# First norm's scale behind the transposes, handovers without GpSimd, and early splits of the next stage's first weights

## The chip, the cores and the metric

The kernel runs on one core of a Trainium2 chip. The metric is the device time of one execution in microseconds. Before the change it is 1447.9 us, the median of three runs that lie between 1447.25 and 1447.98.

## What is computed

A transformer block and two further layers, over 512 tokens of 1024 float32 features:

```python
def first_block(x, ...):
    h = rms_norm(x, pre_mix_g)                 # x * rsqrt(mean(x*x) + eps) * g
    proj = h @ w_in                            # 1024 x 8192
    ...                                        # two attentions, gated: mix
    x = x + rms_norm(mix @ w_mix_out, post_mix_g)
    h = rms_norm(x, pre_ffn_g)
    u = causal_depthwise_conv(h @ w_up, conv_w, conv_b)
    gate, val = jnp.split(u, 2, axis=-1)
    y = (jax.nn.gelu(gate, approximate=True) * val) @ w_down
    return x + rms_norm(y, post_ffn_g)

def second_block(x, ...):
    for l in range(2):
        h = rms_norm_2(x, norm_pre[l])
        proj = h @ w_in[l]                     # 1024 x 2732
        ...                                    # three attentions: mixed
        x = x + rms_norm_2(mixed @ w_out[l], norm_post[l])
    return x
```

## The kernel before, in words

Every float32 operand of a large product is split in two parts, hi (a cast on ScalarE) and lo (source minus hi, on VectorE); `mm3` then makes three matmuls for one, hi by hi, hi by lo and lo by hi. Weights come by DMA from SyncE's queue into `wraw` (three buffers) and `wsplit` makes `whi` and `wlo` (four buffers each). Activations are normalised with a token on each partition and then transposed on TensorE (`tp`), four tiles of 128 columns into one PSUM bank; `transpose_split` casts that bank into the hi part of `hT` on ScalarE and subtracts into its lo part on VectorE. There are four tiles of 128 tokens, t = 0 to 3, each with two halves of 512 features (u = 0, 1).

A stage ends in `post_norm`: the product with the output weights, for the last four k's held back (`LATE` = 4), so that tile 0 is finished first, then tile 1 and so on. `finish(t)` makes tile t's last products, the mean of squares (ScalarE squares with an accumulator, `mean_squares`; GpSimd makes v and then r = v to the power -1/2), y = product times r times gain (VectorE, one instruction for each half), the residual sum (half 0 on GpSimd, half 1 on VectorE), and then `after`, which is the next stage's `pre_norm`: squares of the sum, v and r, xn = x times r times gain (VectorE), transposes, splits. `in_steps` interleaves the tiles. There are three such handovers into a next stage: from the mix to the FFN, from the FFN to layer 0, from layer 0 to layer 1. `ahead`, set at the end of each `post_norm`, gives the next four weight splits an engine for their lo part: three of four go to GpSimd, and the last two wait until tile 1's hT is made.

The first product after a handover is `fm` for the FFN (a chunk of 128 columns of the gate or value half; the first two chunks in two halves of 256 tokens, so that tiles 0 and 1 suffice to begin) and `tm_full` for a layer (428 columns, two k's for one load).

At the start the gains of the first norm are spread over the partitions by two matmuls with a row of ones (`g_pre`), and matmuls on a zero tile (`keep_busy`, tile `idle`) run before and behind them, to no output. The first product (`pv`) makes the values of the first attention, in fours of 128 tokens.

Each engine takes its instructions in the order that the program has after scheduling, and a waiting instruction holds all behind it on its engine.

Of the kernel before, what the change touches and what calls it, by code (L numbers as in the profile page):

```python
# [94 lines left out]
def emit(tc, A, out):  # L95
# [9 lines left out]
    def f(t):  # L105
        return t.bitcast(F32)
# [77 lines left out]
    def wsplit(raw):  # L184
# [26 lines left out]
    def fm(W, pitch, base, c0, acts, kt=8, tag="pj", parts=1):  # L211

        hi, lo = wsplit(wtile(wcols(W, pitch, base, c0, 128, kt)))
        ps = bank(tag, "fm")
        n = 512 // parts
        for u in range(0, 512, n):
            for k in range(kt):
                ah, al = acts(k)
                mm3(ps[:, u:u + n], hi[:, k], lo[:, k], ah[:, u:u + n], al[:, u:u + n],
                    k == 0, k == kt - 1)  # L220
# [11 lines left out]
    def transpose_split(src, k0, t, hT, sp_tag="t"):  # L232
# [9 lines left out]
    def pre_norm(xt, t, g, hT, pool):  # L242
# [4 lines left out]
        for u in range(2):  # L247
            normed[t] = nc.vector.scalar_tensor_tensor(xn[u], xt[u], r, g[u], op0=OP.mult,
                                                       op1=OP.mult).ins
        yield  # L250
        for u in range(2):
            transpose_split(xn[u], u * 4, t, hT, "pj" if t == 1 else "t")
# [33 lines left out]
    def tm_full(W, pitch, base, kt, acts, tags, c0, w, kstep):  # L286

        banks = [bank(tg, "tm") for tg in tags]
        for s in range(0, kt, kstep):
            hi, lo = wsplit(wtile(wrows(W, pitch, base, s, kstep, c0, w)))  # L290
            for k in range(kstep):
                ah, al = acts(s + k)
                for t in range(4):
                    mm3(banks[t][:, :w], ah[:, t * 128:(t + 1) * 128],
                        al[:, t * 128:(t + 1) * 128], hi[:, k], lo[:, k],
                        s + k == 0, s + k == kt - 1)
        return banks

    def post_norm(W, base, kt, act, g, resid, pool, after, last=False):
# [23 lines left out]
        def finish(t):  # L323
# [978 lines left out]
```

## Time and profile before

| what | value |
|---|---|
| time, median of three runs | 1447.9 us |
| profiled execution's own time | 1448.2 us |
| its span, first to last instruction | 1446.4 us |
| TensorE busy | 1428.5 us, 99% of the span |
| VectorE busy | 805.8 us, 56% |
| ScalarE busy | 635.1 us, 44% |
| GpSimd busy | 119.5 us, 8% |
| mean granted TensorE clock | 0.998 |

The profiled execution is one run of the same program. PE is TensorE, DVE is VectorE, ACT is ScalarE, POOL is GpSimd, SP is SyncE. Behind an operation stand the tile that it writes and those that it reads; a line number is that of the program. In a timeline, what stands in brackets is the idle time in front of an instruction and the instruction that ended it. A float32 matmul on the idle tile, and one that spreads the gains, leaves two records in the trace.

### The profile page before, as it was taken

The page shows a single profiled execution, that of the slowest core. Times are in us where ns is not written, and L with a number is a line of the kernel's source. Part 1 is how long each engine was busy: PE and PEld are TensorE (multiplying, and loading weights), DVE is VectorE, ACT ScalarE, POOL GpSimd, SP SyncE. Part 2 cuts the span into 40 slices and gives each one's busy share as a digit, 9 for nine tenths or more (in the row PEclk, how much of TensorE's full clock was granted, in tenths as well). Part 3 has the DMA queues.
Part 4 walks back from the last instruction along what each step waited for, and adds up shares of the span by engine and source line. Part 5 has one row for each costly group of instructions (what it writes and reads, how often), then busy time and mean ns, then how long its engine had stood idle before and what let it go on. Part 6 is the DMA issues. An engine that isn't in the chain of part 4 may idle for free.

```text
span 1446.4 us, 19576 instructions
## 1 busy us (share of the span) xinstructions
PE 1428.5 (99%) x7384; PEld 1153.2 (80%) x7384; DVE 805.8 (56%) x1559; ACT 635.1 (44%) x1346; POOL 119.5 (8%) x188
## 2 busy tenths in 40 slices
PE   9999999999999999999999999999999989999998
PEld 7778878887888888888888888876777777767776
DVE  6454367555434465655554335657666376575745
ACT  4444443333322354433333324536666353475643
POOL 1000000000000060000000004500000064000000
PEclk9999999999999999999999999999999999999999
DMA  5664345432333526433342332633111315311111
GB/s 180 169 170 118 86 110 140 108 94 74 106 101 97 176 75 108 117 102 91 99 131 87 102 97 64 182 105 88 30 45 59 101 46 121 80 44 44 59 45 73
DMA packets 212360, 141.91 MB, mean 98 GB/s; under 512 B 39383, under 2 KB 191971, under 8 KB 212266
## 3 DMA queue, kind: packets, MB, share of 16 engines
q1 hardware_dynamic: 212266, 140.67, 35.1%
q8 instruction: 58, 0.95, 0.3%
q14 instruction: 36, 0.29, 0.1%
HBM read 129.08 MB, written 5.00 MB: 93 GB/s over the span
## 4 chain that ended last, share of the span: by engine, by line
PE 93%; POOL 3%; DVE 1%; ACT 1%; DMA 1%; issue 1%; SPq 0%; DVEq 0%; POOLq 0%; ACTq 0%
PE fm L207 17%; PE fm L208 17%; PE fm L209 17%; PE tm L207 6%; PE tm L209 6%; PE tm L208 6%; PE pt L861 3%; PE pv L207 2%; PE pv L209 2%; PE pv L208 2%; PE oA L866 2%; PE S L948 1%; PE S L1166 1%; PE S L949 1%; PE oC L866 1%; PE oM L866 1%
## 5 line engine op out<-in xcount | busy, mean ns | idle before, releaser
L207 PE MATMUL fm<-hT,whi 128*128 128x512 f32 (+1 forms) x1056 | 407.4, 386 | 1.5 <-DVE hT L175 1.4
L208 PE MATMUL fm<-hT,whi 128*128 128x512 f32 (+1 forms) x1056 | 408.0, 387 | 0.0
L209 PE MATMUL fm<-hT,wlo 128*128 128x512 f32 (+1 forms) x1056 | 407.2, 386 | 0.0
L175 DVE TENSOR_TENSOR wlo<-wraw,whi 128x1024 fp32r<-128x1024 f32 (+1 forms) x209 | 245.7, 1177 | 259.3 <-ACT whi L174 248.1
L174 ACT CAST whi<-wraw 128x1024 fp32r<-128x1024 f32 (+2 forms) x218 | 219.5, 1009 | 324.0 <-PE fm L208 238.2
L207 PEld LDWEIGHTS fm<-hT,whi 128*128 128x128 f32 x1056 | 198.3, 188 | 41.4 <-DVE hT L175 1.6
L209 PEld LDWEIGHTS fm<-hT,wlo 128*128 128x128 f32 x1056 | 198.6, 188 | 39.8 <-issue 1.8
L208 PEld LDWEIGHTS fm<-hT,whi 128*128 128x128 f32 x1056 | 198.7, 188 | 39.3 <-issue 1.7
L208 PE MATMUL tm<-wlo,ah 128*128 128x512 f32 x368 | 143.7, 391 | 0.0
L209 PE MATMUL tm<-whi,al 128*128 128x512 f32 x368 | 143.0, 390 | 0.0
L207 PE MATMUL tm<-whi,ah 128*128 128x512 f32 x368 | 139.1, 392 | 0.0
L864 ACT COPY PT<-pt 128x512 f32<-128x512 f32 (+1 forms) x104 | 51.3, 521 | 79.5 <-PE pt L861 73.8
L207 PEld LDWEIGHTS tm<-whi,ah 128*128 128x128 f32 x368 | 69.1, 188 | 14.6 <-issue 0.7
L209 PEld LDWEIGHTS tm<-whi,al 128*128 128x128 f32 x368 | 69.1, 188 | 14.3 <-issue 0.2
L208 PEld LDWEIGHTS tm<-wlo,ah 128*128 128x128 f32 x368 | 69.1, 188 | 14.0
L272 POOL TENSOR_SCALAR post_v<-post_ss 128x1 f32<-128x1 f32 x16 | 9.3, 583 | 763.0 <-ACT y L268 642.3
L789 DVE SCALAR_TENSOR_TENSOR u<-fm,cw,u 128x511 f32<-128x511 f32 x88 | 65.4, 746 | 8.6 <-ACT u L786 7.2
L891 ACT ACTIVATE P<-P,nm 128x256 f32<-128x256 f32 (+3 forms) x96 | 53.5, 561 | 21.7 <-DVE nm L887 21.4
L861 PE MATMUL pt<-ident,P 128*128 128x128 f32 x352 | 56.7, 284 | 0.0
L861 PEld LDWEIGHTS pt<-ident,P 128*128 128x128 f32 x352 | 38.0, 141 | 20.2 <-issue 18.2
L207 PE MATMUL pv<-whi,hT 128*128 128x512 f32 x128 | 51.3, 406 | 0.0
L209 PE MATMUL pv<-whi,hT 128*128 128x512 f32 x128 | 51.2, 403 | 0.0
(280 smaller groups left out, 1948.5 us busy)
## 6 DMA issues: line engine op xcount, KB each, us to landing
wraw<-in_w_in_dram SPq DMA_DIRECT2D x100, 512.0 KB, 4.3
wraw<-in_w_up_dram SPq DMA_DIRECT2D x44, 512.0 KB, 4.0
wraw<-in_w_down_dram SPq DMA_DIRECT2D x22, 512.0 KB, 3.6
wraw<-in_w_out_dram SPq DMA_DIRECT2D x16, 512.0 KB, 3.5
rs<-rq SPq DMA_DIRECT2D x48, 128.0 KB, 2.3
xt<-in_x_dram SPq DMA_DIRECT2D x16, 256.0 KB, 6.4
wraw<-in_w_mix_out_dram SPq DMA_DIRECT2D x8, 512.0 KB, 3.9
w<-in_cmp_w_dram SPq DMA_DIRECT2D x32, 128.0 KB, 3.6
```

The source lines that it names most:

```text
L174: a = nc.scalar.copy(hi, src)
L175: return a, engine.tensor_tensor(out=lo, in0=src, in1=f(hi), op=OP.subtract)
L207: nc.tensor.matmul(ps, ah, bh, start=first, stop=False)
L208: nc.tensor.matmul(ps, ah, bl, start=False, stop=False)
L209: nc.tensor.matmul(ps, al, bh, start=False, stop=last)
L789: nc.vector.scalar_tensor_tensor(u[:, d:], ps[:, :T - d], cw[:, j, c:c + 1], u[:, d:], op0=OP.mult, op1=OP.add)
L861: nc.tensor.transpose(pt[:, o + i * 128:o + i * 128 + 128], p, ident)
L864: nc.scalar.copy(at[:, :o], pt[:, :o])
L866: nc.tensor.matmul(O[ROWS[r], c0:c0 + w], v(r, kb), at[:, o:o + w], start=start, stop=stop)
L891: nc.scalar.activation(t[:, c:c + w], t[:, c:c + w], AF.Exp, bias=nm[:, u:u + 1], scale=-1.0, accum_out=den[:, u:u + 1])
L948: nc.tensor.matmul(ps[:, :w], q[:, s], kh[:, k0:k0 + w], start=True, stop=False)
L949: nc.tensor.matmul(ps[:, :w], q[:, s], kl[:, k0:k0 + w], start=False, stop=True)
```

## The change

- **The start.** The gains are loaded as eight rows of 128, transposed once to a column for each block of 128 features (`gT`), and multiplied in behind the transposes: xn is now only x times r (half 0 a copy with a scale on ScalarE, half 1 on VectorE), and VectorE multiplies the transposed bank by the columns back into xn, from where hT's parts are split. The row of ones, the two spreading matmuls and the eight idle matmuls behind them go; the idle matmuls at the head become twelve in place of nine.
- **The handovers.** The residual sum of half 0 moves from GpSimd to VectorE, and all weight splits have their lo part on VectorE. Nothing waits for tile 1's hT any more.
- **Early splits.** Ahead of `finish`, the first weights of the next stage (chunk 0 of gate and value for the FFN; k = 0 to 3 of the 428 columns for a layer) are loaded and split into tiles `wh` and `wl` that lie with the activations, so that they don't take the four held buffers. The other weights are split as before.

```diff
     def wsplit(raw):
...
-        engine, t = ahead.pop(0) if ahead else (nc.vector, None)
-        with ExitStack() as queued:
-            for ins in evacuated[t] if t is not None else ():
-                queued.enter_context(tc.issue_after(ins))
-            split(raw, hi, lo, engine)
+        split(raw, hi, lo)
         return hi, lo
...
+    def split_k(src, hi, lo):
+        hi, lo = [a[:, :src.shape[1] * src.shape[2]].rearrange("p (k n) -> p k n", k=src.shape[1])
+                  for a in (hi, lo)]
+        split(src, hi, lo)
+        return [(hi[:, k], lo[:, k]) for k in range(src.shape[1])]
...
     def transpose_split(src, k0, t, hT, sp_tag="t", gT=None):
...
+        if gT is not None:
+            h = src.rearrange("p (a b) -> p a b", a=4)
+            i = nc.vector.tensor_tensor(
+                h, ps, gT[:, k0:k0 + 4][:, :, None].to_broadcast([128, 4, 128]), op=OP.mult)
+            scaled.setdefault(t, []).append(i.ins)
+            ps = h
...
     def pre_norm(xt, t, g, hT, pool, gT=None):
...
+        if gT is None:
+            for u in range(2):
+                nc.vector.scalar_tensor_tensor(xn[u], xt[u], r, g[u], op0=OP.mult, op1=OP.mult)
+        else:
+            scaled[t] = [nc.scalar.activation(xn[0], xt[0], AF.Copy, scale=r).ins]
+            nc.vector.tensor_scalar(xn[1], xt[1], r, None, op0=OP.mult)
...
         def finish(t):
...
-                    (nc.vector if u else nc.gpsimd).tensor_tensor(out=res[u], in0=res[u],
-                                                                  in1=ys[u], op=OP.add)
+                    nc.vector.tensor_add(res[u], res[u], ys[u])
...
+        first = ready()
         in_steps([finish(t) for t in range(4)], SKEW)
-        ahead[:] = [(nc.gpsimd, None), (nc.gpsimd, None), (nc.vector, 1), (nc.gpsimd, 1)]
+        return first
...
-    keep_busy(9)
+    keep_busy(12)
     xt = [load_x(0)]
...
-    for u in range(2):
-        spread = nc.tensor.matmul(g_pre[u], grow[:, D:], grow[:, u * 512:u * 512 + 512],
-                                  start=True, stop=True)
-    with tc.issue_after(spread.ins):
-        keep_busy(8)
+    ps = bank("t", "gT")
+    nc.tensor.transpose(ps[:, 0:8], g8, ident[0:8, 0:8])
+    gT = small("gT", 8, 1)
+    nc.vector.tensor_copy(gT, ps[:, 0:8])
...
+    def up_weights():
+        res = []
+        for c0 in (0, DFF):
+            raw = wtile(wcols(A["w_up"], 2 * DFF, 0, c0, 128))
+            res.append(split_k(raw[:, 0:4], c2("wh", F32R), c2("wl", F32R))
+                       + split_k(raw[:, 4:8], c2("wh", F32R), c2("wl", F32R)))
+        return res
...
+    def layer_weights(l):
+        res = []
+        for k0 in (0, 2):
+            raw = wtile(wrows(W2, PW2, l * D * PW2, k0, 2, A_G, 428))
+            for k in range(2):
+                res += split_k(raw[:, k:k + 1], c2("wh", F32R), c2("wl", F32R))
+        return res
```

How the instructions stand: at the start, on TensorE, before the change (`tp_161` and `tp_168` are tile 0's two banks, `tp_186` is tile 1's first; a row with x8 stands for eight alike):

```order
L381 MATMUL idle_81<-z_80 128x128 x9
L397 MATMUL g_pre_103<-grow_97 128x512 x2
L381 MATMUL idle_81<-z_80 128x128 x8
L236 MATMUL tp_161<-ident_72,xn_136 128x128 x4
L236 MATMUL tp_168<-ident_72,xn_137 128x128 x4
L236 MATMUL tp_186<-ident_72,xn_145 128x128 x4
L207 MATMUL pv_240<-whi_242,hT0_78 128x512
L208 MATMUL pv_240<-wlo_243,hT0_78 128x512
L236 MATMUL tp_193<-ident_72,xn_146 128x128 x4
L209 MATMUL pv_240<-whi_242,hT1_79 128x512
```

and with it (`tp_156` and `tp_164` are tile 0's banks, `tp_183` is tile 1's first):

```order
L399 MATMUL idle_81<-z_80 128x128 x12
L413 MATMUL gT_105<-ident_72,g8_100 128x8
L240 MATMUL tp_156<-ident_72,xn_131 128x128 x4
L240 MATMUL tp_164<-ident_72,xn_132 128x128 x4
L200 MATMUL pv_243<-whi_245,hT0_78 128x512
L201 MATMUL pv_243<-wlo_246,hT0_78 128x512
L202 MATMUL pv_243<-whi_245,hT1_79 128x512
...
L200 MATMUL pv_243<-whi_261,hT0_78 128x512
L240 MATMUL tp_183<-ident_72,xn_140 128x128 x4
```

The gain matmuls and eight idle ones are gone, tile 0's first six products stand ahead of tile 1's transposes, and the second weights (`whi_261`) come before those.

At the handover to the FFN, on VectorE, from tile 2's y on, before (`xt` is the residual; `hT1` is the lo part of hT, from tile 0's two banks and then tile 1's two):

```order
L347 SCALAR_TENSOR_TENSOR y_4282<-tm_3970,post_r_4291,g_post_3944 128x512
L347 SCALAR_TENSOR_TENSOR y_4283<-tm_3971,post_r_4291,g_post_3944 128x512
L349 TENSOR_TENSOR xt_3957<-xt_3957,y_4283 128x512
L175 TENSOR_TENSOR hT1_3965<-tp_4231,hT0_3964 128x4x128
L175 TENSOR_TENSOR hT1_3965<-tp_4238,hT0_3964 128x4x128
L175 TENSOR_TENSOR hT1_3965<-tp_4293,hT0_3964 128x4x128
L175 TENSOR_TENSOR hT1_3965<-tp_4300,hT0_3964 128x4x128
```

and with the change (`wlo_4542` and `wlo_4601` are chunk 1's gate and value weights, `wlo_4663` is chunk 2's gate; `tp_4254` and `tp_4261` are tile 0's banks, `tp_4316` is tile 1's first):

```order
L365 SCALAR_TENSOR_TENSOR y_4305<-tm_3973,post_r_4314,g_post_3947 128x512
L365 SCALAR_TENSOR_TENSOR y_4306<-tm_3974,post_r_4314,g_post_3947 128x512
L172 TENSOR_TENSOR wlo_4542<-wraw_4539,whi_4541 128x1024
L367 TENSOR_TENSOR xt_3959<-xt_3959,y_4305 128x512
L367 TENSOR_TENSOR xt_3960<-xt_3960,y_4306 128x512
L172 TENSOR_TENSOR wlo_4601<-wraw_4598,whi_4600 128x1024
L172 TENSOR_TENSOR wlo_4663<-wraw_4660,whi_4662 128x1024
L172 TENSOR_TENSOR hT1_3968<-tp_4254,hT0_3967 128x4x128
L172 TENSOR_TENSOR hT1_3968<-tp_4261,hT0_3967 128x4x128
L172 TENSOR_TENSOR hT1_3968<-tp_4316,hT0_3967 128x4x128
L172 TENSOR_TENSOR hT1_3968<-tp_4323,hT0_3967 128x4x128
L259 SCALAR_TENSOR_TENSOR xn_4334<-xt_3959,pre_r_4365,g_ffn_3949 128x512
```

Three weight splits and one more add stand ahead of hT's first lo part. The first product of the FFN reads the lo parts of tile 0 and tile 1 out of the first bank of each.

At the handover to layer 1, on VectorE, from tile 1's xn on, before:

```order
L248 SCALAR_TENSOR_TENSOR xn_9612<-xt_3952,pre_r_9643,g_pre_9325 128x512
L248 SCALAR_TENSOR_TENSOR xn_9613<-xt_3953,pre_r_9643,g_pre_9325 128x512
L349 TENSOR_TENSOR xt_3957<-xt_3957,y_9646 128x512
L175 TENSOR_TENSOR hT1_9328<-tp_9594,hT0_9327 128x4x128
L175 TENSOR_TENSOR hT1_9328<-tp_9601,hT0_9327 128x4x128
L175 TENSOR_TENSOR hT1_9328<-tp_9656,hT0_9327 128x4x128
L175 TENSOR_TENSOR hT1_9328<-tp_9663,hT0_9327 128x4x128
```

and with the change (`y_9684` and `y_9685` are tile 2's y, `wlo_9889` holds k = 6 and 7, `wlo_10058` and `wlo_10162` are weights of the next product):

```order
L259 SCALAR_TENSOR_TENSOR xn_9651<-xt_3955,pre_r_9682,g_pre_9344 128x512
L259 SCALAR_TENSOR_TENSOR xn_9652<-xt_3956,pre_r_9682,g_pre_9344 128x512
L367 TENSOR_TENSOR xt_3959<-xt_3959,y_9684 128x512
L172 TENSOR_TENSOR wlo_9889<-wraw_9886,whi_9888 128x856
L367 TENSOR_TENSOR xt_3960<-xt_3960,y_9685 128x512
L172 TENSOR_TENSOR wlo_10058<-wraw_10055,whi_10057 128x1024
L365 SCALAR_TENSOR_TENSOR y_9746<-tm_9354,post_r_9755,g_post_9342 128x512
L365 SCALAR_TENSOR_TENSOR y_9747<-tm_9355,post_r_9755,g_post_9342 128x512
L172 TENSOR_TENSOR wlo_10162<-wraw_10159,whi_10161 128x1024
L172 TENSOR_TENSOR hT1_9347<-tp_9633,hT0_9346 128x4x128
L172 TENSOR_TENSOR hT1_9347<-tp_9640,hT0_9346 128x4x128
L172 TENSOR_TENSOR hT1_9347<-tp_9695,hT0_9346 128x4x128
```

Here too three weight splits, an add and tile 3's y stand ahead of hT's lo parts, which stood behind one add.

## Rows read from the trace of the kernel before

**Rows 1.** The page's first lines: span, and busy time with instruction counts.

```profile
span 1446.4 us, 19576 instructions
...
PE 1428.5 (99%) x7384; PEld 1153.2 (80%) x7384; DVE 805.8 (56%) x1559; ACT 635.1 (44%) x1346; POOL 119.5 (8%) x188
```

**Rows 2.** What TensorE waited for, whole run: total us, times, longest.

```profile
PE tp L236 <- DVE xn L248: 4.5, 3, 2.9
...
PE kr L1001 <- POOL cn L997: 0.7, 1, 0.7
```

**Rows 3.** Timeline of TensorE, start: start, length, operation, count.

```profile
1.07 4.21 PE L381 MATMUL idle<-z 128*128 128x128 f32 x18 [1.07 <-DVE z L374]
...
5.21 3.78 PE L397 MATMUL g_pre<-grow 1*128 1x512 f32 x4
...
8.92 3.78 PE L381 MATMUL idle<-z 128*128 128x128 f32 x16
...
12.49 2.15 PE L236 MATMUL tp<-ident,xn 128*128 128x128 f32 x12
...
14.40 0.49 PE L207 MATMUL pv<-whi,hT 128*128 128x512 f32 x1
```

**Rows 4.** Timelines of ScalarE, VectorE, GpSimd in the first 12 us.

```profile
7.67 1.04 ACT L174 CAST whi<-wraw 128x1024 fp32r<-128x1024 f32 x1 [2.36 <-DMA wraw<-in_w_in_dram]
...
9.24 0.61 ACT L268 ACTIVATE xn<-xt 128x512 f32<-128x512 f32 x1
...
9.21 1.40 DVE L248 SCALAR_TENSOR_TENSOR xn<-xt,pre_r,g_pre 128x512 f32<-128x512 f32 x2 [8.04 <-PE g_pre L397]
...
10.53 1.22 DVE L175 TENSOR_TENSOR wlo<-wraw,whi 128x1024 fp32r<-128x1024 f32 x1
...
5.79 0.57 POOL L274 TENSOR_TENSOR pre_r<-pre_v,mhalf 128x1 f32<-128x1 f32 x1
```

**Rows 5.** Timelines at the handover to the FFN: TensorE, VectorE, GpSimd.

```profile
529.95 0.39 PE L207 MATMUL fm<-hT,whi 128*128 128x256 f32 x1
...
531.77 0.39 PE L207 MATMUL fm<-hT,whi 128*128 128x256 f32 x1 [1.43 <-DVE hT L175]
...
516.52 1.41 DVE L347 SCALAR_TENSOR_TENSOR y<-tm,post_r,g_post 128x512 f32<-128x512 f32 x2 [7.46 <-POOL post_r L274]
...
527.04 1.41 DVE L347 SCALAR_TENSOR_TENSOR y<-tm,post_r,g_post 128x512 f32<-128x512 f32 x2 [0.46 <-POOL post_r L274]
...
529.84 1.87 DVE L175 TENSOR_TENSOR hT<-tp,hT 128x512 fp32r<-128x512 f32 x3
...
520.99 1.29 POOL L349 TENSOR_TENSOR xt<-xt,y 128x512 f32<-128x512 f32 x1 [0.53 <-DVE y L347]
```

**Rows 6.** Timelines at the handover to layer 0: TensorE, VectorE.

```profile
899.70 0.46 PE L208 MATMUL tm<-wlo,hT 128*128 128x428 f32 x1 [1.26 <-POOL wlo L175]
...
894.01 1.41 DVE L347 SCALAR_TENSOR_TENSOR y<-tm,post_r,g_post 128x512 f32<-128x512 f32 x2 [0.46 <-POOL post_r L274]
```

**Rows 7.** Timelines at the handover to layer 1: TensorE, VectorE.

```profile
1165.73 1.03 PE L236 MATMUL tp<-ident,xn 128*128 128x128 f32 x8
...
1169.72 0.66 PE L236 MATMUL tp<-ident,xn 128*128 128x128 f32 x4 [2.95 <-DVE xn L248]
...
1173.03 0.56 PE L209 MATMUL tm<-whi,hT 128*128 128x428 f32 x1
...
1174.64 0.36 PE L208 MATMUL tm<-wlo,hT 128*128 128x428 f32 x1
...
1167.47 3.88 DVE L248 SCALAR_TENSOR_TENSOR xn<-xt,pre_r,g_pre 128x512 f32<-128x512 f32 x2
...
1171.28 0.68 DVE L349 TENSOR_TENSOR xt<-xt,y 128x512 f32<-128x512 f32 x1
```

**Rows 8.** One window, 1171 to 1174 us: busy by engine, clock, DMA.

```profile
1171.00:1174.00 3.00, 2.59 (x9) 2.49 (x10) 3.00 (x6) 1.44 (x3) 1.60 (x2) 0.50 0.49 143
```

More of the change, by code (lines that the diff above doesn't have):

```diff
@@ L163, in emit, with split @@
     nc.vector.memset(mhalf, -0.5)
-    ahead = []
-    evacuated, normed = {}, {}
+    evacuated, scaled = {}, {}
     queued = []
-    def split(src, hi, lo, engine=nc.vector):
+    def split(src, hi, lo):
         a = nc.scalar.copy(hi, src)
-        return a, engine.tensor_tensor(out=lo, in0=src, in1=f(hi), op=OP.subtract)
+        return a, nc.vector.tensor_tensor(out=lo, in0=src, in1=f(hi), op=OP.subtract)
     def wtile(src3):
@@ L209, in mm3, with fm @@
         nc.tensor.matmul(ps, al, bh, start=False, stop=last)
-    def fm(W, pitch, base, c0, acts, kt=8, tag="pj", parts=1):
-        hi, lo = wsplit(wtile(wcols(W, pitch, base, c0, 128, kt)))
+    def split_k(src, hi, lo):
[3 more added lines that the diff above has]
+        return [(hi[:, k], lo[:, k]) for k in range(src.shape[1])]
+    def fm(W, pitch, base, c0, acts, kt=8, tag="pj", parts=1, first=None):
+        if first is None:
+            hi, lo = wsplit(wtile(wcols(W, pitch, base, c0, 128, kt)))
+            first = [(hi[:, k], lo[:, k]) for k in range(kt)]
         ps = bank(tag, "fm")
@@ L284, in gain, with tm_full @@
         return [g[:, u:u + 512] for u in (0, 512)]
-    def tm_full(W, pitch, base, kt, acts, tags, c0, w, kstep):
+    def tm_full(W, pitch, base, kt, acts, tags, c0, w, kstep, first):
         banks = [bank(tg, "tm") for tg in tags]
         for s in range(0, kt, kstep):
-            hi, lo = wsplit(wtile(wrows(W, pitch, base, s, kstep, c0, w)))
+            if s < len(first):
+                ws = first[s:s + kstep]
+            else:
+                hi, lo = wsplit(wtile(wrows(W, pitch, base, s, kstep, c0, w)))
+                ws = [(hi[:, k], lo[:, k]) for k in range(kstep)]
             for k in range(kstep):
@@ L294, in tm_full, with post_norm @@
                     mm3(banks[t][:, :w], ah[:, t * 128:(t + 1) * 128],
-                        al[:, t * 128:(t + 1) * 128], hi[:, k], lo[:, k],
-                        s + k == 0, s + k == kt - 1)
+                        al[:, t * 128:(t + 1) * 128], *ws[k], s + k == 0, s + k == kt - 1)
         return banks
-    def post_norm(W, base, kt, act, g, resid, pool, after, last=False):
+    def post_norm(W, base, kt, act, g, resid, pool, after, last=False, ready=lambda: None):
         banks = [[bank(a, "tm"), bank(b, "tm")] for a, b in
@@ L406, in emit @@
     va = [c2("va") for _ in range(4)]
-    in_steps([pre_norm(xt[t], t, g_pre, hT, mp) for t in range(4)], 1)
+    in_steps([pre_norm(xt[t], t, None, hT, mp, gT) for t in range(4)], 1)
     spill = [dp.tile([4, 128, 640], F32, name="spill0"), dp.tile([8, 128, 384], F32, name="spill1")]
@@ L453, in tm_cols @@
                         if c0 == VA and not k0:
-                            behind.enter_context(tc.issue_after(normed[0]))
+                            for i in (scaled[0][0], scaled[0][-1]):
+                                behind.enter_context(tc.issue_after(i))
                         ws[k0] = wsplit(raw)
@@ L818, in emit @@
     A_Q, A_KV, A_G, C_Q, C_KV, Z = 0, 256, 640, 1068, 1580, 1708
+    def layer_weights(l):
[5 more added lines that the diff above has]
+        return res
+    first = post_norm(A["w_down"], 0, NF, lambda k: yT[k], g_post, lambda t: xs[t], fp,
+                      lambda t, d: pre_norm(d, t, g_pre, hT, fp), ready=lambda: layer_weights(0))
+    fp_stack.close()
+    lt = root.enter_context(tc.tile_pool(name="lt", bufs=1, reuse_waits="tile"))
     lp = None
@@ L952, in emit, with layer @@
     ROWS = (slice(0, 64), slice(64, 128))
-    def layer(l):
+    def layer(l, first):
         nonlocal lp
@@ L1258, in emit @@
     for l in range(2):
-        mixed = layer(l)
+        mixed = layer(l, first)
         pn_stack, pn = phase("pn%d" % l, jy=6, xn=6)
```

40 lines of the change are left out of this document (17 added, 23 removed).

## The prediction

> **What bounds the kernel now.** I read the page first: TensorE is busy 1428.5 of a span of 1446.4 us [rows 1], so at most 17.9 us of the span can be won by ending its idle time. The profiled execution took 1448.2, which is 1.8 outside the span and 0.3 over the median of 1447.9; the sum below is made against it, and its difference is then laid on the median. The view of waits says where TensorE stood still in the places that the change touches: 4.5 us in three waits for xn and, a little later, 0.7 for kr [rows 2], 1.4 for a hT split [rows 5] and 1.3 for a weight split on GpSimd [rows 6]. The timelines of the start and of the three handovers give the rest. The reader is to see three things in them. At the start the first product stands at 14.40, after 12.5 us of work that gives no output [rows 3]. At a handover VectorE and ScalarE take their queues in order, so that what ends TensorE's wait is the instruction of theirs that comes last in the queue. And a long wait costs more than itself: after 2.95 us without work the 428-column products took 0.56 instead of 0.36 us [rows 7], and the granted clock was 0.50 from 1171 to 1174 [rows 8].
>
> **The start.** Removed are the two gain matmuls (3.78 us as four records), a memset, a 4 KB load and eight idle matmuls (3.57 us, 16 records, two for each) [rows 3]; added are three idle matmuls, an 8x128 load, one transpose of 8 columns with a copy of its result, and eight multiplications of 128x512. VectorE's first xn waited 8.04 us for the gains and began at 9.21, though rstd was there at 6.36 [rows 4]. The twelve idle matmuls end near 1.07 + 12 x 0.47 = 6.7. xn of tile 0 would be ready near 7.0, its eight transposes (0.13 to 0.18 each) near 8.3, and two multiplications (the trace has none out of PSUM by a broadcast column; I take 0.7, half of an xn pair's 1.40 [rows 4], as it also has two operands of that size, with 0.62 of a hT split out of PSUM [rows 5] and 0.75 as bounds) near 9.3. Then ScalarE has the squares of tile 1 ahead (they end near 9.95 [rows 4]), so hT's first cast is done at 10.5 and the first product stands at 10.6: a lead of 3.8 us.
>
> Most of the lead can't be kept, because the supply has not moved. Weights and x tiles land when they did, and ScalarE has one queue for all of it: two hT casts to 11.0, the second whi (1.04 [rows 4]) to 12.05, a square of tile 2 and the copy that is now half of tile 1's xn (0.6 each) to 13.2, then a square, a whi, two squares of tile 3 and the copy for tile 2's xn, 3.5 together, to 16.7. With six products from 11.2, six more after the transposes near 14.3, five after 17.8 and fourteen until 22.1, I count 32 products of 0.2275 us done at 22.1 in the new order, against 27 in the old one ((22.1 - 14.40 - 1.5 for transposes)/0.2275). Five products are 1.1 us. But the clock speaks against all of it: through 12.5 us the idle matmuls ran at 0.47 each, and twelve transposes took 0.18 each where eight later take 0.13 [rows 3, 7], so TensorE was at the lower level while it was busy without a gap; with gaps at 8.5 to 10.6 and at 12.3 I let the first dozen products take twice their time; most of that falls into the waits for supply, and the count leaves two to four products. I take **-0.8**; bounds -3.8 (whole lead kept) and +1.5 (lower level until about 20).
>
> **The handover to the FFN.** GpSimd's add of 1.29 us [rows 5] stands in its queue between the small operations that make rstd, so without it rstd comes about 1.7 us sooner and VectorE's y pair of tile 2 begins near 525.3 instead of 527.04. What follows is fixed by the order: before one add and then hT's low halves, the third of which ended at 531.71 and released TensorE at 531.77 [rows 5]; now a weight split (1.2 [rows 4]), two adds (0.65 each, from the 0.68 of an add that ran alone [rows 7]), two more weight splits, and only then hT. So 525.3 + 1.35 + 1.2 + 1.3 + 2.4 + three hT of 0.62 = 533.4: **+1.7** for TensorE. The splits that gained a place are those of chunk 1, which nobody needs for some 5 us; chunk 0's, which are made early, were not what TensorE waited for here. ScalarE's third cast waits until tile 3's product frees a buffer, and is done at 527.7, when the first transposes end, so it costs nothing; if it were late, each hT cast would be late by as much. The wait grows to 3.3 us at one piece, longer than the 2.95 after which the products slowed. There some eight products at the lower level cost 8 x 0.16 = 1.3; I take **+1.1** for the same here (bounds 0 and 1.5).
>
> **The handover to layer 0.** The y pair begins 1.7 sooner than 894.01, near 892.3, then 1.35, a split of 856 columns (1.0), two adds (1.3), another 1.0, a split of 1024 (1.2), and the first hT (0.62): 898.8. TensorE has four products by then; before it had seven and went on at 899.70 [rows 6]. Three products are 0.6, so this gives **-0.3** (bounds -1.3, the whole wait, and +0.3).
>
> **The handover to layer 1.** The xn pair of tile 1 took 3.88 us, beside a GpSimd split and add [rows 7]; the pair at the start took 1.40 [rows 4]. It now begins 1.6 earlier (no add in GpSimd's queue) and takes 1.4, so it ends at 1167.3 instead of 1171.35, and the transposes are over by 1167.8. The Trainium skill ("GPSIMD Engine Reference", section 1, the specifications) says that GpSimd shares its SBUF interfaces with VectorE and that VectorE instructions with two SBUF inputs contend; the trace agrees, with 3.88 beside GpSimd and 1.40 without.
>
> But behind that pair VectorE's queue now has an add (0.65), a split (1.0), an add, a split of 1024 (1.2), the y pair of tile 3 (1.35), a third split (1.2) and then the first hT (0.62): 1174.0. Before, the first hT came right after the xn pair and one add. So TensorE has its transposes and four products done and stands until 1174.0, while before it had eight products done at 1174.4, the dip behind it. Four products more are 0.8, so it is 0.4 later in work, and a dip as long as the old one is still to come (+1.3). Given back are the last of the three xn waits (4.5 - 2.95 - 0.64 = 0.9 [rows 2, 7]), and I take half of kr's wait, as GpSimd is free (-0.3). Sum **+0.5**, bounds -1.2 (no dip, kr's 0.7 gone) and +1.8 (a third early weight lands 0.8 late, the dip half a microsecond longer).
>
> The early splits themselves go into the long product stage ahead, where VectorE had nothing to do for 7.46 us [rows 5]; I cost them at nothing there, and at up to 1 us if a weight's landing stood in front of ScalarE's first squares.
>
> **Sum.** -0.8 + 1.7 + 1.1 - 0.3 + 0.5 = +2.2 us; 1450.4 against 1448.2, and on the median **1450.1**.
>
> **Rivals.** What a measurement here can tell is about 0.2%, 2.9 us: between 1445.0 and 1450.8 is no change.
>
> *The clock falls and stays down longer (slower).* After waits of 3.3 us at the FFN and over 4 us in front of 1174, and the gaps of the start, TensorE works for twice as long at the lower level. Priced: start +0.5 in place of -0.8, FFN +1.7 + 2.2, layer 0 -0.3, layer 1 +1.6: +5.7, 1453.6. For it speaks the one dip in the trace, which followed the longest wait [rows 7, 8]; against it, that it ended by itself within 3 us. It decides early: 0.7 us more at the lower level than I count, and the sum is beyond 2.9. The Trainium skill ("TensorE: Matmul & The Clock Gate", Part 1, on oscillation) warns of idle gaps between bursts of matmuls as what drops the clock; the dip at 1171 agrees.
>
> *The order does not bind (faster).* If the hT splits were not held by the weight splits in front, the waits of 1.4, 1.3 and 4.5 and the dip's 1.3 would nearly go, with the start -0.8: about -9, 1439. Against it: the engines run their queue in order, and the three splits are there in the printed order at all three places; the time in front of them is filled with work whose durations are measured. It would need VectorE ready some 3.5 us earlier at the FFN.
>
> *The lead of the start is kept (faster by little).* -3.8 in place of -0.8 makes the sum -0.8, 1447.1: still within no change, and faster only if both dips stay out as well (-3.2).
>
> *It does not do what it says.* The early weights are ready but unused, since hT is what is missing: that is my own sum; with no dip at all it is -0.2, 1447.7.
>
> **How the numbers follow.** My forecast (no change, a little slower in the middle): 0.42, which takes in the kept lead and the sum without a dip. The clock: 0.38 for slower. Faster by either way: 0.20. The range goes from 1444.7, where the kept lead without dips ends, to 1453.6, where the clock's rival ends; what is left out is the order that doesn't bind (about 0.1) and a sum of all worse bounds (0.1). The forecast's own range is 1447 to 1451.
>
> **What would show it.** Right: first product near 10.6 but gaps on TensorE until 18; one wait of about 3.3 us at the FFN, ended by hT; no xn wait at layer 1 but one wait of over 4 us for hT; xn pairs of 1.4 everywhere; GpSimd with rstd only. Wrong: waits there under 1.5 us, or hT ahead of the splits in time. A stall on a raw weight's landing on ScalarE would be a cost that I put at nothing.

## The result: 0.9% slower, and the profile after

The changed kernel took 1459.82 us (median of 5 runs, 1459.45 to 1460.58) beside 1447.25 us (5 runs, 1447.08 to 1447.98) of the kernel before: a ratio of 1.0090, 95% interval [1.0078, 1.0101]. That is 12.6 us more, against a forecast of +2.2 us, and 6.2 us above the upper end of the range. The profiled execution has a span of 1457.7 us, 11.3 more than before [rows 1].

The first lines of the page of the changed kernel:

```profile
span 1457.7 us, 19614 instructions
...
PE 1430.1 (98%) x7371; PEld 1155.3 (79%) x7371; DVE 812.5 (56%) x1590; ACT 638.4 (44%) x1356; POOL 82.1 (6%) x167
```

GpSimd has lost 37 us of work and VectorE has gained 7. TensorE's busy time has grown by 1.6 us, in which the matmuls that the start lost and the slow products behind the waits stand against each other; the other 9.7 of the 11.3 us are idle time on TensorE. The view of waits says where (total us, times, longest):

```profile
PE tm L202 <- DVE hT L172: 5.6, 2, 4.3
PE fm L200 <- DVE hT L172: 4.2, 1, 4.2
PE ctp L1037 <- DVE cn L1022: 2.3, 3, 1.4
PE tp L240 <- ACT xn L261: 1.9, 1, 1.9
PE tp L240 <- DVE xn L259: 1.6, 1, 1.6
PE pv L200 <- ACT hT L171: 1.1, 1, 1.1
```

The three waits for xn of [rows 2] have shrunk from 4.5 to 1.6, as wanted. In their place stand waits for hT of 4.2 and 4.3, one of 1.4 in the same row as the 4.3 (at layer 0), and three for cn, a row in which the kernel before has one wait of 0.6.

How far behind each stretch has left the kernel is read by putting the same product (the nth matmul of a tile name) of both traces side by side. Differences in us, worked out from the two timelines; minus is sooner than before. "Start" ends near 299 us of the kernel before, "gates" near 529, the FFN's handover and FFN at 845, layer 0's handover at 1004, layer 1's handover at 1280; between 1004 and 1164 and behind 1280 all kernels move by 0.2 or less. Each row is one execution, the profiled one, and can lie up to 1.5 us off its kernel's median (e11's is the lowest of eleven, 1446.78 beside 1448.23).

| kernel | start | gates | FFN | layer 0 | layer 1 | span |
|---|---|---|---|---|---|---|
| forecast | -0.8 | 0 | +2.8 | -0.3 | +0.5 | +2.2 |
| changed | 0.0 | +1.0 | +3.7 | +4.8 | +2.2 | +11.3 |
| e1_hT_first | -0.8 | +1.0 | +1.1 | +1.3 | -0.3 | +2.0 |
| e2_nopool_alone | +0.1 | +0.1 | +3.6 | -0.3 | -3.6 | -0.1 |
| e3_early_alone | -1.3 | +0.1 | +2.0 | +1.7 | -1.1 | +1.4 |
| e4_start_alone | +0.1 | +1.0 | -0.3 | 0.0 | -0.5 | 0.0 |
| e5_warm | -0.5 | +1.0 | +1.3 | +4.9 | +2.4 | +8.6 |
| e6_handovers_alone | -0.1 | +0.1 | +3.4 | +4.7 | +2.6 | +10.8 |
| e7_strict | +0.1 | 0.0 | -1.4 | +1.2 | -1.7 | -1.9 |
| e8_ffn_early | -1.2 | +0.1 | -1.2 | -0.5 | -3.3 | -6.1 |
| e9_late0 | -0.9 | +1.0 | +3.5 | -0.3 | +3.3 | +6.4 |
| e10_fast_early0 | -0.5 | 0.0 | -1.7 | +4.8 | -3.5 | -0.8 |
| e11_fast_early1 | -1.3 | 0.0 | -1.6 | -0.1 | +1.2 | -1.7 |

**The start.** Timeline of TensorE in the changed kernel (start, length):

```profile
1.07 4.84 PE L399 MATMUL idle<-z 128*128 128x128 f32 x24 [1.07 <-DVE rb L430]
5.84 0.22 PE L413 MATMUL gT<-ident,g 8*128 8x8 f32 x1
8.00 1.55 PE L240 MATMUL tp<-ident,xn 128*128 128x128 f32 x8 [1.94 <-ACT xn L261]
10.68 0.80 PE L200 MATMUL pv<-whi,hT 128*128 128x512 f32 x1 [1.12 <-ACT hT L171]
11.47 0.79 PE L201 MATMUL pv<-wlo,hT 128*128 128x512 f32 x1
...
15.94 0.40 PE L202 MATMUL pv<-whi,hT 128*128 128x512 f32 x1
```

The first product stands at 10.68 and not at 14.40 [rows 3], a lead of 3.7 us. At 34 us 0.15 of it is left, at 299 us nothing.

**The handover to the FFN.** Timelines of TensorE, VectorE and ScalarE, and two windows (their columns: bounds, length, busy time and count of TensorE, its weight loads, VectorE, ScalarE, GpSimd, then the granted clock, DMA share and GB/s):

```profile
535.37 0.58 PE L200 MATMUL fm<-hT,wh 128*128 128x256 f32 x1 [4.23 <-DVE hT L172]
535.75 0.42 PE L201 MATMUL fm<-hT,wh 128*128 128x256 f32 x1
535.97 0.42 PE L202 MATMUL fm<-hT,wl 128*128 128x256 f32 x1
...
527.50 1.41 DVE L365 SCALAR_TENSOR_TENSOR y<-tm,post_r,g_post 128x512 f32<-128x512 f32 x2 [0.46 <-POOL post_r L287]
...
533.44 2.47 DVE L172 TENSOR_TENSOR hT<-tp,hT 128x512 fp32r<-128x512 f32 x4
...
528.80 1.55 ACT L171 CAST hT<-tp 128x512 fp32r<-128x512 f32 x3
...
534.00:541.00 7.00, 5.63 (x26) 5.63 (x27) 6.89 (x11) 0.89 (x1) 1.19 (x3) 0.51 0.49 140
940.00:944.00 4.00, 3.64 (x10) 3.00 (x11) 3.88 (x6) 1.07 (x2) 1.70 (x5) 0.57 0.13 17
```

One wait of 4.23 us has taken the place of 1.43 [rows 5], and behind it the 256-column products follow each other at 0.21 us with the clock at 0.51, its lower level of 1.2 GHz, until 541 (such a stretch is called a dip below). ScalarE's first three casts of hT end at 530.35, three us before VectorE takes up its part, so it is VectorE's queue that holds the product.

**The handover to layer 0.** TensorE's wait, and ScalarE's first instructions of the norm of cq and ckv (ct is the copy of one tile's result out of PSUM, cj its squares):

```profile
904.68 0.46 PE L202 MATMUL tm<-wh,hT 128*128 128x428 f32 x1 [1.35 <-DVE hT L172]
...
920.76 0.63 PE L200 MATMUL fm<-hT,whi 128*128 128x512 f32 x2
921.23 0.35 PE L202 MATMUL tm<-wh,hT 128*128 128x428 f32 x1
...
926.58 1.05 ACT L171 CAST whi<-wraw 128x1024 fp32r<-128x1024 f32 x1 [5.57 <-PE tm L202]
927.78 0.52 ACT L1008 COPY ct<-tm 128x428 f32<-128x428 f32 x1
928.20 0.42 ACT L1018 ACTIVATE cj<-ct 128x256 f32<-128x256 f32 x1
```

In the kernel before the same two, the last tile's copy and the first squares behind it, stand here:

```profile
919.81 0.52 ACT L971 COPY ct<-tm 128x428 f32<-128x428 f32 x1
920.22 0.42 ACT L981 ACTIVATE cj<-ct 128x256 f32<-128x256 f32 x1
```

The squares start 8.0 us later, of which the kernel brought 4.7 along. The reason begins at 920.76 on TensorE: matmuls of the next product (fm) stand between those of the 428-column product (tm), two here and nine from 923.54, together 2.5 us, where the kernel before has none. So its last tile ends late, and all four tiles' squares are behind that tile's copy in ScalarE's queue. At the transposes of cn TensorE then waits for 0.56, 0.35 and 1.36 us, 2.3 in all, and the clock falls once more (0.57 over the window from 940, above).

**The handover to layer 1.** Timelines of TensorE and VectorE:

```profile
1177.62 1.32 PE L240 MATMUL tp<-ident,xn 128*128 128x128 f32 x8 [1.61 <-DVE xn L259]
...
1184.63 0.72 PE L202 MATMUL tm<-wh,hT 128*128 128x428 f32 x1 [4.27 <-DVE hT L172]
1185.16 0.56 PE L200 MATMUL tm<-wh,hT 128*128 128x428 f32 x1
...
1189.44 0.40 PE L200 MATMUL tm<-whi,hT 128*128 128x428 f32 x1
...
1176.82 1.41 DVE L259 SCALAR_TENSOR_TENSOR xn<-xt,pre_r,g_pre 128x512 f32<-128x512 f32 x2
...
1183.90 2.48 DVE L172 TENSOR_TENSOR hT<-tp,hT 128x512 fp32r<-128x512 f32 x4
```

The xn pair takes 1.41 and not 3.88 [rows 7]; but hT comes 7 us behind it, and 13 products run at 0.36 us each.

### The profile page after: what moved, and what is told of

Read it like the earlier page. It is cut to its first block, busy times and chain, and to the rows that moved or that the text cites. A ratio compares the mean times of both kernels' runs of the same rounds, so it can differ in the third digit from the quotient of the medians.

```text
span 1457.7 us, 19614 instructions
## 1 busy us (share of the span) xinstructions
PE 1430.1 (98%) x7371; PEld 1155.3 (79%) x7371; DVE 812.5 (56%) x1590; ACT 638.4 (44%) x1356; POOL 82.1 (6%) x167
## 4 chain that ended last, share of the span: by engine, by line
PE 67%; issue 25%; POOL 3%; DVE 2%; ACT 2%; DMA 1%; SPq 0%; POOLq 0%; DVEq 0%; ACTq 0%
PE fm L200 11%; PE fm L201 11%; PE fm L202 11%; PE pt L897 3%; PE tm L202 3%; PE tm L200 3%; PE tm L201 3%; PE pv L202 2%; PE pv L200 2%; PE pv L201 2%; PE oA L902 2%; PE S L984 1%; PE S L1203 1%; PE S L985 1%; PE oC L902 1%
## 5 line engine op out<-in xcount | busy, mean ns | idle before, releaser
L201 PE MATMUL fm<-hT,whi 128*128 128x512 f32 (+1 forms) x1024 | 399.5, 390 | 0.0
L200 PE MATMUL fm<-hT,whi 128*128 128x512 f32 (+1 forms) x1024 | 399.2, 390 | 0.0
L202 PE MATMUL fm<-hT,wlo 128*128 128x512 f32 (+1 forms) x1024 | 398.8, 390 | 0.0
L172 DVE TENSOR_TENSOR wlo<-wraw,whi 128x1024 fp32r<-128x1024 f32 (+2 forms) x212 | 248.8, 1175 | 254.9 <-ACT whi L171 249.7
L171 ACT CAST whi<-wraw 128x1024 fp32r<-128x1024 f32 (+2 forms) x212 | 213.7, 1010 | 323.4 <-PE fm L201 238.4
L200 PEld LDWEIGHTS fm<-hT,whi 128*128 128x128 f32 x1024 | 192.7, 188 | 40.1 <-issue 1.5
L202 PEld LDWEIGHTS fm<-hT,wlo 128*128 128x128 f32 x1024 | 192.8, 188 | 38.8 <-issue 1.2
L201 PEld LDWEIGHTS fm<-hT,whi 128*128 128x128 f32 x1024 | 192.9, 188 | 38.5 <-issue 0.8
```

The lines of the kernel that those rows point to most:

```text
L172: return a, nc.vector.tensor_tensor(out=lo, in0=src, in1=f(hi), op=OP.subtract)
L200: nc.tensor.matmul(ps, ah, bh, start=first, stop=False)
L201: nc.tensor.matmul(ps, ah, bl, start=False, stop=False)
L202: nc.tensor.matmul(ps, al, bh, start=False, stop=last)
```

## The experiments

The theory after the result: VectorE's early queue is what costs. The early weights let the later weight splits stand ahead of hT, the work taken from GpSimd stands there too, and each long wait for hT drops the clock. Its rivals: one part alone is to blame; the loss is the start's; or the waits cost and the clock adds nothing.

**e1: hT's two parts ahead of the weight splits.** From the changed kernel; held back are the splits' casts on ScalarE and their low halves on VectorE:

```diff
-        split(raw, hi, lo)
+        t = ahead.pop(0) if ahead else None
+        with ExitStack() as behind:
+            for ins in evacuated[t] if t is not None else ():
+                behind.enter_context(tc.issue_after(ins))
+            split(raw, hi, lo)
...
         in_steps([finish(t) for t in range(4)], SKEW)
+        ahead[:] = [] if last else [1, 1, 1]
```

> The changed kernel, with the three weight splits behind each handover put behind tile 1's hT splits on both engines. Order theory (the loss of 12.6 us is made by these splits standing ahead of hT): most of it goes, 1448 to 1452; at the FFN some stays, since tile 2's xn pair now stands ahead of hT's third part. VectorE-load theory (GpSimd's work costs VectorE the same wherever it stands): 1456 or more.

Measured: 1450.95 us, ratio to before 1.0027 [1.0016, 1.0038]. Holding three weight splits back behind hT of tile 1 gives back 8.9 of the 12.6 us. The order in the queues of VectorE and ScalarE is most of the loss. At the FFN one wait of 1.5 is left and at layer 1 one of 2.3, both for ScalarE's part of hT. In layer 0 the long wait for hT is gone and the waits for cn remain (waits between 885 and 950 us):

```profile
PE ctp L1043 <- DVE cn L1028: 1.9, 2, 1.4
PE ctp L1043 <- DVE cn L1030: 0.4, 1, 0.4
PE tm L205 <- ACT hT L172: 0.2, 1, 0.2
```

**e2: GpSimd's sums and splits on VectorE, and nothing else.** From the kernel before:

```diff
-                    (nc.vector if u else nc.gpsimd).tensor_tensor(out=res[u], in0=res[u],
-                                                                  in1=ys[u], op=OP.add)
+                    nc.vector.tensor_add(res[u], res[u], ys[u])
...
-        ahead[:] = [(nc.gpsimd, None), (nc.gpsimd, None), (nc.vector, 1), (nc.gpsimd, 1)]
+        ahead[:] = [(nc.vector, None), (nc.vector, None), (nc.vector, 1), (nc.vector, 1)]
```

> The kernel before, with only GpSimd's sums and weight splits moved to VectorE, no early splits, old start. Order theory: two splits stand ahead of hT at the FFN and one at each layer, so about half of the loss: 1450 to 1454. VectorE-load theory: nearly the whole loss, 1456 or more. If the early splits are what costs: 1447 to 1449.

Measured: 1446.64 us, ratio 0.9996 [0.9987, 1.0004]. No change in the whole, but two effects of 3.6 us each that cancel out: lost at the FFN, where TensorE waits for hT and the products behind run slowly, won at layer 1, where the xn pairs run without GpSimd beside them and the longest wait and the dip of [rows 7, 8] are gone. The 1450 to 1454 of the order theory missed, since it has no gain at layer 1. The group view of xn, duration of one in ns (least, median, most), and the wait:

```profile
L248 DVE SCALAR_TENSOR_TENSOR xn<-xt,pre_r,g_pre x24: 739/745/752, 9.2 to 1183.2; 128x512 f32<-128x512 f32 x24
...
533.43 0.58 PE L207 MATMUL fm<-hT,whi 128*128 128x256 f32 x1 [3.20 <-DVE hT L175]
```

In the kernel before the longest of the 24 took 2503 ns.

**e3: the early weights, and nothing else.** From the kernel before, the part of the diff with `first` and `ready`, and:

```diff
-        ahead[:] = [(nc.gpsimd, None), (nc.gpsimd, None), (nc.vector, 1), (nc.gpsimd, 1)]
+        ahead[:] = [(nc.vector, 1), (nc.gpsimd, 1)]
```

> The kernel before, with only the early splits; the sums and every second later split stay on GpSimd, and the later splits wait for tile 1's hT as before. Order theory: no split ahead of hT, so no loss: 1444 to 1449. If the early splits (their loads, their place ahead of the squares) are the cost: 1452 or more.

Measured: 1449.81 us, ratio 1.0023 [1.0014, 1.0032], between the two that were expected. It loses 2.0 at the FFN, where hT's cast on ScalarE is late (a wait of 2.6), and 1.7 at layer 0, where the three waits for cn have the 2.3 us of the changed kernel. So the cn waits come from the early weights, with GpSimd still at work.

**e4: the start, and nothing else.** From the kernel before, the part of the diff with `gT` and `g8`, twelve idle matmuls, and the wait on `scaled`:

```diff
-    g_pre = bank_pair("g_pre")
...
+    nc.tensor.transpose(ps[:, 0:8], g8, ident[0:8, 0:8])
+    gT = small("gT", 8, 1)
+    nc.vector.tensor_copy(gT, ps[:, 0:8])
```

> The kernel before with only the new start. By the lag of the same products in the two traces the start is worth 0.0 at 212 us: 1447 to 1449. If the start also makes the scheduler interleave the two gate products, which lost 0.9 us between 370 and 480 us: 1448 to 1449. By my prediction's term: 1446.5.

Measured: 1447.29 us, ratio 1.0001 [0.9993, 1.0010]. The start is worth nothing either way. The three parts alone (e4, e2, e3) make +0.2, -0.4 and +2.8 us beside the 1447.06 of the kernel before in these runs; 2.6 in all, where the change makes 12.6. That does not show that the parts fail to add up, since one part is in none of the three: in each of them two weight splits still wait for tile 1's hT, as in the kernel before, and in the change nothing does. e1, the changed kernel with such a wait on three splits, lies 3.9 above the kernel before.

**e5: TensorE kept busy through the FFN's wait.** From the changed kernel; the products of the identity with itself add work whose result is overwritten (18 float32 products, which leave 36 records):

```diff
         ps = bank(tag, "fm")
+        if warm:
+            with tc.issue_after(warm_after[0]):
+                for _ in range(warm):
+                    nc.tensor.matmul(ps[:, :128], ident, ident, start=True, stop=True)
...
-                parts=2 if c < 2 else 1, first=None if c else first[1])
+                parts=2 if c < 2 else 1, first=None if c else first[1], warm=0 if c else 18)
```

> The changed kernel with 18 products of the identity with itself, to no output, in TensorE's wait of 4.2 us at the handover to the FFN. Clock theory: the 29 products of 256 columns that took 0.213 us each behind that wait take 0.12, so 2.5 to 2.8 us come back: 1456.8 to 1457.5. If the clock is set by something else than TensorE's idle time: 1459.5 or more, the rows behind the wait still at 0.41.

Measured: 1456.80 us, ratio 1.0065 [1.0052, 1.0077], 3.0 below the changed kernel; between the two traces the FFN's stretch gives back 2.4. hT comes when it did. What is gone is the dip:

```profile
530.26 4.18 PE L223 MATMUL fm<-ident 128*128 128x128 f32 x36
...
534.91 0.39 PE L201 MATMUL fm<-hT,wh 128*128 128x256 f32 x1 [0.22 <-DVE hT L173]
535.13 0.28 PE L202 MATMUL fm<-hT,wh 128*128 128x256 f32 x1
535.25 0.28 PE L203 MATMUL fm<-hT,wl 128*128 128x256 f32 x1
```

The products follow each other at 0.12 us and not at 0.21. The granted clock is 1.00 from 525 to 545 us. So the clock's fall is a cost of its own, about 2.5 us at this one place. The Trainium skill ("TensorE: Matmul & The Clock Gate", Part 1, on oscillation) warns of idle gaps between bursts of matmuls as what brings the lower clock; this run agrees, with 1.00 where the wait is filled and 0.51 where it is not.

**e6: the handovers, and nothing else.** The changed kernel with the start of the kernel before:

```diff
-    keep_busy(12)
+    keep_busy(9)
...
-    nc.tensor.transpose(ps[:, 0:8], g8, ident[0:8, 0:8])
...
+    g_pre = bank_pair("g_pre")
```

> The changed kernel with the old start. If the start is worth nothing by itself and the loss is all in the handovers: 1457.5 to 1460; the 0.9 us between 370 and 480 us gone if it came with the new start. If new start and handovers need each other for the loss: under 1455.

Measured: 1459.22 us, ratio 1.0078 [1.0065, 1.0091]. All three handovers cost what they cost in the changed kernel. The +1.0 us in the gates is gone: it belongs to the new start.

**e7: the whole order strict.** e6 with e1's edit, and tile 2's sums held back in the same way, at all handovers:

```diff
-                    nc.vector.tensor_add(res[u], res[u], ys[u])
+                    with ExitStack() as behind:
+                        for ins in evacuated[1] if t == 2 and not last else ():
+                            behind.enter_context(tc.issue_after(ins))
+                        nc.vector.tensor_add(res[u], res[u], ys[u])
```

> The changed kernel with the old start, the three weight splits behind tile 1's hT, and tile 2's sums behind it too. Order theory: the FFN's wait all but gone there (lag at the FFN 0 or less, against 1.1 in the first such run); the layers still lose 1 to 2 us to the later norm chain, since next products stand ahead of the tail of the 428-column product. Sum 1445.5 to 1449. VectorE-load theory: not under 1450.

Measured: 1446.58 us, ratio 0.9991 [0.9983, 1.0000]. 12.6 us below e6 by waits in the queues of VectorE and ScalarE alone, the same work on the same engines. There is no dip left but that at the end. Layer 0 still costs 1.2.

**e8: early weights at the FFN only.** From the kernel before: e2's edit, the early weights and e7's order at the FFN, the old order at the two layers:

```diff
+                        for ins in evacuated[1] if t == 2 and pool is mx and not last else ():
...
-        ahead[:] = [(nc.gpsimd, None), (nc.gpsimd, None), (nc.vector, 1), (nc.gpsimd, 1)]
+        ahead[:] = [(nc.vector, 1)] * 3 if kt == 8 and base == 0 and last is False and pool is mx else [(nc.vector, None), (nc.vector, None), (nc.vector, 1), (nc.vector, 1)]
...
+    first = post_norm(A["w_down"], 0, NF, lambda k: yT[k], g_post, lambda t: xs[t], fp,
+                      lambda t, d: pre_norm(d, t, g_pre, hT, fp), ready=lambda: [])
```

> GpSimd out of all handovers, early splits at the FFN alone with hT first there, none at the layers (the old order with VectorE in GpSimd's place), old start. If each handover's effect is its own: FFN 0 or less, layer 0 -0.3, layer 1 -3.6 by the run without GpSimd: 1442.5 to 1444.5, faster than both kernels. If what is won at layer 1 hangs on what stands ahead of it: 1446 to 1448.

Measured: 1442.25 us, ratio 0.9964 [0.9950, 0.9977]: 5.0 us faster than the kernel before and 17.6 faster than the changed one, 0.25 under what was expected. Three windows, one at each handover:

```profile
530.00:536.00 6.00, 6.00 (x53) 6.00 (x52) 5.24 (x7) 3.82 (x11) 3.07 (x4) 1.00 0.49 140
895.00:901.00 6.00, 5.23 (x26) 4.57 (x26) 5.55 (x8) 4.47 (x12) 3.01 (x4) 1.00 0.55 160
1165.00:1173.00 8.00, 6.31 (x32) 5.44 (x33) 7.84 (x12) 4.34 (x9) 3.50 (x4) 1.00 0.26 68
```

In the FFN's window TensorE does not stop at all; the clock is 1.00 in all three.

**e9: layer 0 put back.** From the changed kernel with e1's edit of `wsplit`, to tell whether layer 0's loss is its own or comes from what went before; no weight is split early there, and two of the four splits wait for hT again:

```diff
+        ahead[:] = [None, None, 1, 1] if first == [] else []
...
-                      lambda t, d: pre_norm(d, t, g_pre, hT, fp), ready=lambda: layer_weights(0))
+                      lambda t, d: pre_norm(d, t, g_pre, hT, fp), ready=lambda: [])
```

> The changed kernel with one handover put back: at layer 0 no weight is split early, and the four splits of 856 columns stand where the kernel before has them (two free, two behind the evacuation of tile 1, all on VectorE). Theory A (at layer 0 the early weights themselves cost: with them the next product's matmuls are mixed into the 428-column tail, the norm of cq and ckv starts late, TensorE waits 2.3 us for cn, and the clock falls behind it): the stretch from the end of the down projection to layer 0's attention goes from +4.7 us against the kernel before to between -0.5 and +0.5, the waits of ctp for cn from 2.3 to under 1, and the time from 1459.8 to 1454.5-1456. Theory B (the loss there comes from what the change did earlier, the long wait and dip at the FFN, or from GpSimd's work moved to VectorE): the stretch stays at +3 or more, the time at 1458 or more.

Measured: 1454.72 us, ratio 1.0053 [1.0040, 1.0065]. Layer 0 goes from +4.8 to -0.3 behind the same wait and dip at the FFN, and one wait for cn of 0.6 is left there, as in the kernel before. The loss there is that handover's own.

**e10: the fastest kernel with layer 0's early weights.** From e8, with the changed kernel's order at layer 0 (no split waits for hT there):

```diff
-                      lambda t, d: pre_norm(d, t, g_pre, hT, fp), ready=lambda: [])
+                      lambda t, d: pre_norm(d, t, g_pre, hT, fp), ready=lambda: layer_weights(0))
```

> The fastest kernel so far (e8_ffn_early, 1442.3) with one thing added: layer 0's early weights and its handover in the order of the changed kernel. Theory A (the early weights at layer 0 cost by themselves): +3 to +5 us, 1445-1447.3, with 2.3 us of waits of ctp for cn where e8 has 0.3, and one or two waits for hT before it. Theory B (they cost only behind the FFN's dip): under +1 us, below 1443.3.

Measured: 1447.40 us, ratio 1.0002 [0.9993, 1.0011]; 5.1 above e8, 0.1 above the upper end of what was expected. Layer 0 goes from -0.5 to +4.8, as in the changed kernel. The cn waits are back, beside e8's 0.3:

```profile
PE ctp L1038 <- DVE cn L1023: 1.9, 2, 1.4
...
PE ctp L1038 <- DVE cn L1025: 0.4, 1, 0.4
...
922.49 0.52 ACT L1009 COPY ct<-tm 128x428 f32<-128x428 f32 x1
922.91 0.42 ACT L1019 ACTIVATE cj<-ct 128x256 f32<-128x256 f32 x1
```

In e8 the same squares start at 917.61, 5.3 us sooner. Of the 5.3 some 1.1 are longer waits for hT (0.58 and 1.36, where e8 has 0.6 and 0.2), 1.7 the ten products behind them that follow each other at 0.36 in place of 0.20, since the clock falls (0.50 from 899 to 902), and 2.5 the eleven matmuls of the next product that stand between here too.

**e11: the fastest kernel with layer 1's early weights.** From e8 (and no split waits for hT at layer 1):

```diff
-                          lambda: [])
+                          (lambda: None) if l else lambda: layer_weights(1))
```

> The same kernel (e8_ffn_early, 1442.3) with layer 1's early weights and its handover in the order of the changed kernel, nothing at layer 0. Theory A (VectorE's three weight splits and two adds stand ahead of the first hT there, and the wait drops the clock): a wait for hT of about 4 us and products at twice their time behind it, +5 to +6 us, 1447.2-1448.5. Theory B (there they pay once GpSimd is out): no more than 1 us above e8.

Measured: 1448.23 us, ratio 1.0007 [0.9998, 1.0016]; 6.0 above e8, and 4.5 at layer 1 between the two traces. The wait and the slow products are those of the changed kernel, with nothing lost ahead of them:

```profile
1171.44 0.72 PE L209 MATMUL tm<-wh,hT 128*128 128x428 f32 x1 [4.13 <-DVE hT L175]
1171.96 0.56 PE L207 MATMUL tm<-wh,hT 128*128 128x428 f32 x1
```

## Why the prediction was wrong

**The mechanism was right at the FFN and at layer 1.** hT ended every long wait, from behind the weight splits in VectorE's queue. e7 undoes it by order alone. The rival "the order does not bind" is refuted by that. The rival "the clock falls and stays down longer" named what happened at the FFN and at layer 1, but its sum of +5.7 was less than half of what came, since it left layer 0 at -0.3.

**Layer 0 failed outright: -0.3 forecast, +4.8 measured.** The sum ended at the first hT. The step that failed is "The early splits themselves go into the long product stage ahead ... I cost them at nothing there": they are not paid there but behind the handover, with 2.3 us. With two of four weight tiles out of the way, ScalarE takes up the next product's 1024-column splits early (from 898.66; in the kernel before, from 916.28), and eleven matmuls of that product stand inside the 428-column product, 2.5 us. So the norm of cq and ckv, which the transposes of cn need, begins 2.7 us later within its stage (8.0 less the 4.7 brought along and the 0.6 by which the two waits for hT, 0.54 and 1.35, exceed the old one of 1.26 [rows 6]), and the waits for cn grow from 0.6 to 2.3.

Two more parts make up the 4.8. The products behind the first hT stand 0.9 later than before, not 0.3 sooner: VectorE's y pair begins at 898.35, which is 893.7 without the lag, where the sum has 892.3. And the products at 940 follow each other at 0.43 in place of 0.23, 1.5 us, a dip of which the sum has none here. So 2.3 + 0.9 + 1.5 = 4.7.

e1, e3 and e10 bear this out. In e1 and e3 hT comes early at layer 0 and the clock does not fall there: their lag in this stage is -1.0 and -0.6 behind the first hT and +1.3 and +1.7 at its end, again 2.3 us, with the same eleven matmuls inside and the same 2.3 us of waits for cn. In e2, e8 and e9, without early weights here, it is -0.3 behind hT and -0.3 to -0.5 at the end. In e10 it is +2.4 behind hT, where its dip lies, and +4.8 at the end. e9 and e10 take and give 5 us by the early weights and the order of this handover together.

**The FFN was mis-sized: +2.8 forecast, +3.7 measured.** The chain of durations behind the y pair was right. It begins at 527.50 and the third hT ends at 535.3, 7.8 us later, where the sum has 8.1. Wrong was that the pair begins 1.7 sooner. It stands 0.5 sooner, with the 1.0 that the gates lost taken off. Timelines of VectorE, ScalarE and GpSimd in the changed kernel:

```profile
522.17 1.28 DVE L367 TENSOR_TENSOR xt<-xt,y 128x512 f32<-128x512 f32 x2
...
522.88 0.64 ACT L281 ACTIVATE xn<-xt 128x512 f32<-128x512 f32 x1 [2.04 <-DVE xt L367]
...
524.13 0.58 ACT L281 ACTIVATE y<-tm 128x512 f32<-128x512 f32 x1
...
525.68 0.86 POOL L285 TENSOR_SCALAR post_v<-post_ss 128x1 f32<-128x1 f32 x1
526.63 0.84 POOL L287 TENSOR_TENSOR post_r<-post_v,mhalf 128x1 f32<-128x1 f32 x1
```

The add that left GpSimd is now the second of two on VectorE, and tile 1's squares wait for it; tile 2's squares, which make its rstd, are behind those in ScalarE's queue. GpSimd is idle and yet not sooner, and its two operations of one column still take 0.86 and 0.84 beside VectorE's xn pair. So the wait was 4.23 and not 3.3. The dip was put at 1.1, by eight products, from [rows 7]; it lasted for 24 products of 0.21 in place of 0.12 us and two transposes, 2.5 us with the slower first one, and e5 gets 2.4 back there. The first product behind the wait is 2.6 later (535.37 beside 531.77, less the gates' 1.0). That and the dip make 5.1; 1.4 of it comes back behind, in e5 too (2.7 at the first product, +1.3 at the end), and what gives it back is not shown.

**Layer 1 was mis-sized: +0.5 forecast, +2.2 measured.** The gain was there, xn pairs of 1.41 (the pair at the start, from which the forecast took it, reads its gain out of PSUM, these do not), and e2 shows that it is worth 3.6, the old dip's end included, when hT is not behind splits. A wait for xn of 1.61 stayed, where the forecast has none. The first hT stood at 1184.5, which is 1175.3 with the 9.2 of lag taken off, and not 1174.0: the y pair of tile 2 runs ahead of the xn pair, which begins at 1176.82 and not at its forecast place, 1.7 later. The dip has 13 slow products where the sum has some eight.

**The start's term was too good by 0.8 and cannot be told from none.** The first product stood at 10.68, 10.6 was forecast; the weights, the two waits and the lower clock took the lead away, as the count had it (the products that it lists are 31 and not 32, 0.2 us too good). Measured over kernels, the new start leaves 0.0, -0.8, +0.1, -0.5 and -0.9, the old one +0.1, -1.3, -0.1, +0.1, -1.2, -0.5 and -1.3 beside the kernel before. **The gates' +1.0 had no step**, below.

## What to carry over

When a change makes room in a queue, ask what moves into it: here weight splits that nobody needed yet stood in front of the evacuation (hT's copies out of PSUM) that TensorE waited for, and the cure was to hold the prefetch behind the evacuation, not to make it earlier. Follow an early operand past its first use, to the stage whose queue the next operands then enter; what pays at one handover (the FFN, -1.4 in e7) may cost at the next with the same edit (layer 0, +1.2). Price a long wait with the slow products behind it, counted at its own place. When the parts of a change are tested one by one, see that they make up the whole: here parts of +0.2, -0.4 and +2.8 us stood beside 12.6, because the dropped wait on hT was in none of them.

## What was not expected of the hardware

- **A spread of the start.** With the same instructions the work at 299 us stands up to 1.4 us apart between executions of kernels whose start is the same code (-1.3 to +0.1). It goes with TensorE's pace there: with the old start, the eight idle matmuls behind the gains took 3.78 us in the kernel before, e2, e6 and e7 (lags of -0.1 to +0.1) and 2.05 to 2.78 in e3, e8, e10 and e11 (-1.3 to -0.5), although TensorE was busy without a gap from 1.07 us until their end in all of them. A term under 1 us at the start cannot be read from one trace.
- **The same products at two paces.** In the gates, matmuls of 512 columns follow each other at 0.227 us in the kernel before. In all five kernels with the new start some 18 of every 72 follow at 0.233, at a granted clock of 1.00 and in the same order; in none with the old start. It makes the +1.0 us. What of the new start does it was not tried and stays open.
- **Dips of different length, and not behind each such wait.** Behind waits of 4.23, 4.27 and 4.13 us the products stayed at the lower level for 24 (256 columns, and two transposes), 13 and 13 (428 columns). Behind three short waits of 0.6, 0.4 and 1.4 us with single transposes between them the clock fell too, at 940 us; in e1, e3 and e10 the same three waits, 2.3 us, brought no fall, so one trace does not show what such waits cost.
